# A two-layer decoder trunk: wide products in the query and query-key projections, and a new order of products within a block

## The chip, the cores and the metric

The kernel runs on one core of a Trainium2 chip. The time is device microseconds of one execution. The engines of a core are named as in the profile: PE (TensorE, matrix products) with PEld (its weight loads), DVE (VectorE), ACT (ScalarE), POOL (GpSimd) and SP (SyncE, which issues the loads of weights). SBUF is the memory the engines work from, PSUM the one in which PE sums its products.

## The reference

256 tokens of width 1024 pass two layers. Layer 0 mixes tokens by a recurrence and by retention, layer 1 by differential attention; both go on with a cross-attention into 256 memory tokens and an MLP of width 4096. What matters here, cut to the lines:

```python
# layer 1's mixing
q, k, v = jnp.split(h @ w_in, 3, axis=-1)          # 1024 columns each
...
# both layers
q = (h @ w_q).reshape(bsz, s, X_HEADS, X_HEAD_DIM)
k, v = jnp.split(mem_n @ w_kv, 2, axis=-1)
logits = jnp.einsum('bshd,bmhd->bhsm', q, k).astype(jnp.float32) * (X_HEAD_DIM ** -0.5)
p = jax.nn.softmax(logits, axis=-1)
o = jnp.einsum('bhsm,bmhd->bshd', p.astype(v.dtype), v)
return o.reshape(bsz, s, D_MODEL) @ w_o
...
# both layers
jnp.square(jax.nn.relu(h @ w1)) @ w2
```

## The kernel before

**Products in parts.** Most products are made of two parts of each operand, a high part hi (the value rounded to the type that PE multiplies) and a low part lo (the rest). A product is the sum of three: hi by hi, lo by hi, hi by lo. `split` makes the parts: ACT copies the source into hi, DVE subtracts hi from the source. Both operations have line L129 for every operand.

**Weights.** `wpiece` (L138) loads a piece of 512 KB into `raw` (4 buffers) and splits it into `hi` and `lo` (3 buffers each), at a high priority in the scheduler, which places them ahead of other work that is ready on ACT and DVE. A piece is one block: 128 output columns over all 1024 input rows. A split of 128x1024 can begin when the block three places before has released its buffers.

**Two ways to project.** The activations are held transposed, columns are tokens: `xh` and `xl` of 128 x 8 x 256. `proj_cols` (L163) takes two blocks into one PSUM tile `mm` of 128x512, 256 columns a block: per block and each of the 8 slices kt of the input, three products of 256 columns (narrow: `mm<-xhl,hi`, `mm<-xhl,lo`, `mm<-xhl,hi`), 24 in all. Then one call of `evac` empties the tile. `proj_wide` (L308) takes one block into one tile of 128x512. The hi weights of a slice are multiplied with both parts of the activations in one product of 512 columns (wide), so that hi by hi is summed in the left half and hi by lo in the right half of the tile; the lo weights are multiplied with xh in a narrow product, into the left half. A block has 8 wide and 8 narrow products. Its emptying has to add the halves. In the MLP, `up` (L1003) uses it: ACT copies the right half to `ul` (L1009), DVE adds the left half and `ul` (L1010). A block that comes first after the activations are made (`opening`) is made of 24 narrow products in another order, in both ways.

**Where they are used.** `proj_wide` is used by the MLP's first half in both layers, 32 blocks each, on tiles that alternate between the pools `mm` and `tr` (two buffers each). `proj_cols` is used by `q_proj` in the cross-attention (L924, 4 calls of two blocks per layer) and by the query-key projection of layer 1's differential attention (L1115 and L1116, 8 calls). In layer 0, `q_proj`'s tile is copied whole to `qT` (L927); in layer 1 it is split into two parts `qT`. In the differential attention L1115 and L1116 copy the tile to `qTd` and `kTd`.

**What lies around.** `q_proj` calls alternate with `softmax` of the heads whose queries are ready: scores `acc<-KT,qT`, their maximum and exponential, the reciprocal, the transpositions (`tr`), and the copy or split of the transposed into `PT`. Ahead of it the keys and values of the memory are projected into `mm` tiles; in both layers the last key tile is split into `KT1h` and `KT1l`, and in layer 1 the values are split into `Vs`. In the differential attention each second pair of blocks is followed by `heads` (scores `acc`, a biased copy `z`, maximum, exponential, a weighted difference, transposition `tr`, copy `PTd`).

**What sets the order.** A scheduler places the instructions of each engine in a fixed order from their dependencies and priorities; an engine takes its own in that order. `mm` chains the products of one PSUM bank, so that one sum is not mixed with another. The PSUM pools `acc`, `mm` and `tr` give their buffers in turn: a tile waits until the last reader of the tile two turns before is done (`mm`, `tr`).

Of the kernel before, what the change touches and what calls it, by code (L numbers as in the profile page):

```python
# [8 lines left out]
F32 = mybir.dt.float32  # L9
F32R = mybir.dt.float32r  # L10
AF = mybir.ActivationFunctionType
ALU = mybir.AluOpType
# [25 lines left out]
def kernel(ctx: ExitStack, tc: tile.TileContext, ins: dict, out: bass.AP):  # L38
    nc = tc.nc
    I = ins  # L40
# [5 lines left out]
    const = ctx.enter_context(tc.tile_pool(name="const", bufs=1))  # L46
# [21 lines left out]
    def nm(s):  # L68
        cnt[0] += 1
        return f"{s}_{cnt[0]}"  # L70
# [4 lines left out]
    def mm_t():  # L75
        return ps_mm.tile([128, 512], F32, tag="mm", name=nm("mm"))
# [42 lines left out]
    def mm(o, lhsT, rhs, start, stop):  # L119

        ins = nc.tensor.matmul(o, lhsT=lhsT, rhs=rhs, start=start, stop=stop)  # L121
        key = o.tensor.name
        prev = last_in_bank.get(key)
        if prev is not None:
            behind(ins, prev, "one accumulation group per bank")
        last_in_bank[key] = ins

    def split(hi, lo, src):
        return nc.scalar.activation(hi, src, AF.Copy), nc.vector.tensor_tensor(lo, src, r32(hi), op=ALU.subtract)  # L129
# [178 lines left out]
    def proj_wide(w, blk, xT, ps, opening=False):  # L308

        xh, xl = xT  # L310
        wh, wl = wpiece(w[blk].rearrange("p (kt c) -> p kt c", kt=8), 8, 128)
        if opening:
            for k0 in (0, 4):
                for kt in range(k0, k0 + 4):
                    mm(ps[:, 0, :], lhsT=wh[:, kt, :], rhs=xh[:, kt, :], start=(kt == 0), stop=False)
                    mm(ps[:, 0, :], lhsT=wl[:, kt, :], rhs=xh[:, kt, :], start=False, stop=False)
                for kt in range(k0, k0 + 4):
                    mm(ps[:, 0, :], lhsT=wh[:, kt, :], rhs=xl[:, kt, :], start=False, stop=(kt == 7))
            return False
        for kt in range(8):  # L320
            if kt == 7:
                mm(ps[:, 0, :], lhsT=wl[:, kt, :], rhs=xh[:, kt, :], start=False, stop=False)
            mm(ps, lhsT=wh[:, kt, :], rhs=xT.both[:, kt, :, :], start=(kt == 0), stop=(kt == 7))
            if kt < 7:
                mm(ps[:, 0, :], lhsT=wl[:, kt, :], rhs=xh[:, kt, :], start=False, stop=False)
        return True

    def load_mem(pool):
        mh = pool.tile([128, 8, 256], F32R, tag="memh", name="memh")
# [25 lines left out]
    xT = xt(xpool, "A")  # L355
# [3 lines left out]
    omu = const.tile([128, 14], F32, name="omu")  # L359
    behind(nc.vector.tensor_scalar(omu, prm[:, R_MU:R_MU + 14], -1.0, 1.0, op0=ALU.mult, op1=ALU.add), d1[1], "the activations first")  # L360
    oka = const.tile([128, 4], F32, name="oka")
    const.tile([128, 22], F32, name="pad")

    quad = const.tile([128, 2], F32, name="quad")
    for q in range(4):
# [59 lines left out]
    for b0 in (0, 2):  # L425
# [6 lines left out]
        for j in range(2):  # L432
            b = b0 + j
# [29 lines left out]
    for hf in range(2):  # L463
        for b in range(4):
            mm(pss[:, 0:16].rearrange("p (f h b) -> p f b h", f=2, h=2)[:, hf, b, :],
               lhsT=kk2[:, b, hf * 128:(hf + 1) * 128], rhs=hsel, start=True, stop=True)
# [39 lines left out]
    kT = tok_major(kt_.rearrange("p (b g) t -> p b (g t)", b=4), "kT")  # L506
# [393 lines left out]
    def cross(layer, KT, V, after, mid=lambda: None):  # L900
# [21 lines left out]
        oT = next_xT()  # L922

        def q_proj(c):  # L924
            def ev(ps):
                if layer == 0:
                    nc.scalar.activation(qT[:, 2 * c:2 * c + 2, :], ps, AF.Copy)  # L927
                else:
                    split(qT[0][:, 2 * c:2 * c + 2, :], qT[1][:, 2 * c:2 * c + 2, :], ps)
            proj_cols(I["w_q"][layer], 2 * c, xT, ev, c == 0)  # L930

        def softmax(hp, t):
            ps = acc_t().rearrange("p (h m) -> p h m", h=2)
# [126 lines left out]
    def diff(before, after):  # L1060
# [51 lines left out]
                nc.scalar.activation(PT[:, hd, t * 128:t * 128 + n], pt[:, :n], AF.Copy)  # L1112

        for c in range(4):
            proj_cols(I["w_dqk"], 2 * c, xT, lambda ps, c=c: nc.scalar.activation(qT[:, 2 * c:2 * c + 2, :], ps, AF.Copy), c == 0)  # L1115
            proj_cols(I["w_dqk"], 8 + 2 * c, xT, lambda ps, c=c: nc.scalar.activation(kT[:, 2 * c:2 * c + 2, :], ps, AF.Copy))  # L1116
            if c > 0:
                heads(2 * c - 2)
                heads(2 * c - 1)
# [186 lines left out]
```

## Time and profile before

| what | value |
|---|---|
| runs | 902.22, 899.11, 898.23 us; median 899.11 |
| profiled execution | 897.66 us, its span 895.9 us |
| granted clock of PE, mean | 0.995 |
| instructions in the span | 14122 |
| PE, PEld busy | 876.5, 752.6 us (98%, 84%) |
| DVE, ACT busy | 593.5, 454.9 us (66%, 51%) |
| POOL busy | 30.5 us (3%) |
| HBM read | 148.01 MB, 168 GB/s over the span |

The span runs from the first to the last instruction that the profiler records; the time of an execution holds a little more. PE's records overlap, since the next product enters while the last is still leaving: the time that one takes from the engine is the distance between the starts of two (its pitch), not its duration. A number in brackets behind a row is the idle time of the engine just before it, with what ended it.

By place: layer 0's query projection lies from about 274 to 302 us, its MLP from 340 to 520, layer 1's query-key projection from 530 to 587, its values and output from 587 to 640, its query projection from 649 to 676, its MLP from 712 to 882.

### The profile page before, as it was taken

The page shows a single profiled execution, that of the slowest core. Times are in us where ns is not written, and L with a number is a line of the kernel's source. Part 1 is how long each engine was busy: PE and PEld are TensorE (multiplying, and loading weights), DVE is VectorE, ACT ScalarE, POOL GpSimd, SP SyncE. Part 2 cuts the span into 40 slices and gives each one's busy share as a digit, 9 for nine tenths or more (in the row PEclk, how much of TensorE's full clock was granted, in tenths as well). Part 3 has the DMA queues.
Part 4 walks back from the last instruction along what each step waited for, and adds up shares of the span by engine and source line. Part 5 has one row for each costly group of instructions (what it writes and reads, how often), then busy time and mean ns, then how long its engine had stood idle before and what let it go on. Part 6 is the DMA issues. An engine that isn't in the chain of part 4 may idle for free.

```text
span 895.9 us, 14122 instructions
## 1 busy us (share of the span) xinstructions
PE 876.5 (98%) x5546; PEld 752.6 (84%) x5546; DVE 593.5 (66%) x937; ACT 454.9 (51%) x730; POOL 30.5 (3%) x51
## 2 busy tenths in 40 slices
PE   7999999999999999999999999999999999999996
PEld 5988889777889889888888889978899888888885
DVE  4669888455476557666666675786776676666665
ACT  5765444324465436444444454674564554444443
POOL 2000000001000100000000000001000000000001
PEclk8999999999999999999999999999999999999999
DMA  9754433222656545565555555443563465655551
GB/s 310 237 152 129 140 120 119 72 72 95 198 203 213 185 168 191 195 190 192 193 189 189 188 175 180 142 124 113 170 203 97 153 198 188 188 189 191 188 189 66
DMA packets 47078, 149.98 MB, mean 167 GB/s; under 512 B 4731, under 2 KB 4900, under 8 KB 46884
## 3 DMA queue, kind: packets, MB, share of 16 engines
q1 hardware_dynamic: 45456, 142.73, 49.2%
q10 hardware_dynamic: 1108, 3.72, 1.2%
q0 software_dynamic: 448, 2.63, 0.8%
q8 instruction: 43, 0.70, 0.3%
q14 instruction: 23, 0.19, 0.1%
HBM read 148.01 MB, written 2.63 MB: 168 GB/s over the span
## 4 chain that ended last, share of the span: by engine, by line
PE 90%; DVE 4%; issue 2%; ACT 2%; POOL 1%; DMA 1%; POOLq 0%; SPq 0%; DVEq 0%; ACTq 0%
PE mm L121 37%; PE acc L121 35%; PE tr L121 15%; DVE lo L129 1%; PE tr L254 1%; ACT hi L129 1%; DMA h<-in_x_dram 1%; PE tr L1111 1%; PE tr L958 1%; DVE z L1092 0%; PE acc L254 0%; POOL rs L226 0%; DVE xn L268 0%; PE tr L500 0%; POOL xn L1189 0%
## 5 line engine op out<-in xcount | busy, mean ns | idle before, releaser
L129 DVE TENSOR_TENSOR lo<-raw,hi 128x1024 fp32r<-128x1024 f32 x262 | 320.0, 1223 | 213.3 <-ACT hi L129 211.1
L129 ACT ACTIVATE hi<-raw 128x1024 fp32r<-128x1024 f32 x262 | 277.6, 1060 | 333.5 <-PE mm L121 122.5
L121 PE MATMUL mm<-xhl,hi 128*128 128x256 f32 (+1 forms) x784 | 188.0, 319 | 1.3 <-ACT xhl L129 1.1
L121 PEld LDWEIGHTS mm<-xhl,hi 128*128 128x128 f32 x784 | 129.7, 189 | 12.1 <-ACT xhl L129 2.0
L121 PE MATMUL mm<-xhl,lo 128*128 128x256 f32 x512 | 138.1, 282 | 0.0
L121 PE MATMUL acc<-hi,hl 128*128 128x512 f32 x256 | 100.2, 391 | 0.0
L121 PE MATMUL acc<-hi,hh 128*128 128x512 f32 x256 | 100.1, 391 | 0.0
L121 PE MATMUL acc<-lo,hh 128*128 128x512 f32 x256 | 99.6, 389 | 0.0
L121 PEld LDWEIGHTS mm<-xhl,lo 128*128 128x128 f32 x512 | 96.6, 189 | 2.5
L121 PE MATMUL tr<-xhl,hi 128*128 128x512 f32 x256 | 92.8, 395 | 0.0
L121 PE MATMUL acc<-hi,xhl 128*128 128x512 f32 x256 | 81.9, 396 | 0.0
L121 PE MATMUL tr<-xhl,lo 128*128 128x256 f32 x256 | 66.7, 281 | 0.0
L121 PEld LDWEIGHTS acc<-hi,hl 128*128 128x128 f32 x256 | 48.0, 188 | 11.3 <-DVE hl L129 0.9
L121 PEld LDWEIGHTS acc<-lo,hh 128*128 128x128 f32 x256 | 48.1, 188 | 10.4
L121 PEld LDWEIGHTS acc<-hi,xhl 128*128 128x128 f32 x256 | 47.7, 188 | 9.7
L121 PEld LDWEIGHTS acc<-hi,hh 128*128 128x128 f32 x256 | 48.1, 188 | 8.8
L121 PEld LDWEIGHTS tr<-xhl,hi 128*128 128x128 f32 x256 | 48.2, 188 | 8.5
L121 PEld LDWEIGHTS tr<-xhl,lo 128*128 128x128 f32 x256 | 48.2, 188 | 2.9
L121 PE MATMUL acc<-lo,xhl 128*128 128x512 f32 x128 | 50.4, 394 | 0.0
L121 PE MATMUL mm<-memh,hi 128*128 128x256 f32 x128 | 37.0, 289 | 0.0
L121 PE MATMUL mm<-meml,hi 128*128 128x256 f32 x128 | 36.8, 288 | 0.0
L121 PE MATMUL mm<-memh,lo 128*128 128x256 f32 x128 | 36.5, 285 | 0.0
(303 smaller groups left out, 1369.5 us busy)
## 6 DMA issues: line engine op xcount, KB each, us to landing
raw<-in_w_dram SPq DMA_DIRECT2D x64, 512.0 KB, 4.3
raw<-in_mlp_w_dram SPq DMA_DIRECT2D x64, 512.0 KB, 4.3
raw<-in_hyb_w_in_dram SPq DMA_DIRECT2D x16, 512.0 KB, 3.7
raw<-in_w_k_dram SPq DMA_DIRECT2D x16, 512.0 KB, 3.5
raw<-in_xattn_w_kv_dram SPq DMA_DIRECT2D x16, 512.0 KB, 3.7
raw<-in_w_q_dram SPq DMA_DIRECT2D x16, 512.0 KB, 4.0
raw<-in_xattn_w_o_dram SPq DMA_DIRECT2D x16, 512.0 KB, 3.5
raw<-in_w_dqk_dram SPq DMA_DIRECT2D x16, 512.0 KB, 3.6
```

Source lines behind the costliest of these rows:

```text
L121: ins = nc.tensor.matmul(o, lhsT=lhsT, rhs=rhs, start=start, stop=stop)
L129: return nc.scalar.activation(hi, src, AF.Copy), nc.vector.tensor_tensor(lo, src, r32(hi), op=ALU.subtract)
L254: nc.tensor.transpose(ps[:, k4, :], x[:, kt * 128:(kt + 1) * 128], ident)
L958: nc.tensor.transpose(pt[:, j, m, :], P[:, j, m * 128:(m + 1) * 128], ident)
L1111: nc.tensor.transpose(pt[:, k * 128:(k + 1) * 128], z3[:, 0, k * 128:(k + 1) * 128], ident)
```

## The change

Three things are edited. First, `proj_wide` no longer alternates: it issues seven of the eight wide products, then the eight narrow ones, then the last wide one. Second, a new helper `proj_two` makes two blocks with `proj_wide`, each in an `mm` tile of its own, and hands the left half and the copied right half `ul` to a function `dst`; `q_proj` in both layers and the query-key projection use it in place of `proj_cols`. `summed_to` adds the halves on DVE, or copies an opening block on ACT. In layer 1's `q_proj` the sum is written back to `ul` and then split. With 8 blocks per layer in `q_proj` and 16 in the query-key projection, less the three opening ones, 29 blocks become wide. Third, an unused pad of 22 columns becomes one of 16.

```diff
--- before.py
+++ after.py
@@ -317,13 +317,29 @@
                 for kt in range(k0, k0 + 4):
                     mm(ps[:, 0, :], lhsT=wh[:, kt, :], rhs=xl[:, kt, :], start=False, stop=(kt == 7))
             return False
+        for kt in range(7):
+            mm(ps, lhsT=wh[:, kt, :], rhs=xT.both[:, kt, :, :], start=(kt == 0), stop=False)
         for kt in range(8):
-            if kt == 7:
-                mm(ps[:, 0, :], lhsT=wl[:, kt, :], rhs=xh[:, kt, :], start=False, stop=False)
-            mm(ps, lhsT=wh[:, kt, :], rhs=xT.both[:, kt, :, :], start=(kt == 0), stop=(kt == 7))
-            if kt < 7:
-                mm(ps[:, 0, :], lhsT=wl[:, kt, :], rhs=xh[:, kt, :], start=False, stop=False)
+            mm(ps[:, 0, :], lhsT=wl[:, kt, :], rhs=xh[:, kt, :], start=False, stop=False)
+        mm(ps, lhsT=wh[:, 7, :], rhs=xT.both[:, 7, :, :], start=False, stop=True)
         return True
+
+    def proj_two(w, blk, xT, pool, dst, opening=False):
+
+        for b in range(2):
+            ps = mm_t().rearrange("p (x t) -> p x t", x=2)
+            if proj_wide(w, blk + b, xT, ps, opening and b == 0):
+                ul = pool.tile([128, 256], F32, tag="ul", name=nm("ul"), bufs=2)
+                nc.scalar.activation(ul, ps[:, 1, :], AF.Copy)
+                dst(b, ps[:, 0, :], ul)
+            else:
+                dst(b, ps[:, 0, :], None)
+
+    def summed_to(o, p, ul):
+        if ul is None:
+            nc.scalar.activation(o, p, AF.Copy)
+        else:
+            nc.vector.tensor_tensor(o, p, ul, op=ALU.add)
 
     def load_mem(pool):
         mh = pool.tile([128, 8, 256], F32R, tag="memh", name="memh")
@@ -359,7 +375,7 @@
     omu = const.tile([128, 14], F32, name="omu")
     behind(nc.vector.tensor_scalar(omu, prm[:, R_MU:R_MU + 14], -1.0, 1.0, op0=ALU.mult, op1=ALU.add), d1[1], "the activations first")
     oka = const.tile([128, 4], F32, name="oka")
-    const.tile([128, 22], F32, name="pad")
+    const.tile([128, 16], F32, name="pad")
 
     quad = const.tile([128, 2], F32, name="quad")
     for q in range(4):
@@ -922,12 +938,16 @@
         oT = next_xT()
 
         def q_proj(c):
-            def ev(ps):
+            def dst(b, p, ul):
+                i = 2 * c + b
                 if layer == 0:
-                    nc.scalar.activation(qT[:, 2 * c:2 * c + 2, :], ps, AF.Copy)
+                    summed_to(qT[:, i, :], p, ul)
+                elif ul is None:
+                    split(qT[0][:, i, :], qT[1][:, i, :], p)
                 else:
-                    split(qT[0][:, 2 * c:2 * c + 2, :], qT[1][:, 2 * c:2 * c + 2, :], ps)
-            proj_cols(I["w_q"][layer], 2 * c, xT, ev, c == 0)
+                    summed_to(ul, p, ul)
+                    split(qT[0][:, i, :], qT[1][:, i, :], ul)
+            proj_two(I["w_q"][layer], 2 * c, xT, cp, dst, c == 0)
 
         def softmax(hp, t):
             ps = acc_t().rearrange("p (h m) -> p h m", h=2)
@@ -1112,8 +1132,8 @@
                 nc.scalar.activation(PT[:, hd, t * 128:t * 128 + n], pt[:, :n], AF.Copy)
 
         for c in range(4):
-            proj_cols(I["w_dqk"], 2 * c, xT, lambda ps, c=c: nc.scalar.activation(qT[:, 2 * c:2 * c + 2, :], ps, AF.Copy), c == 0)
-            proj_cols(I["w_dqk"], 8 + 2 * c, xT, lambda ps, c=c: nc.scalar.activation(kT[:, 2 * c:2 * c + 2, :], ps, AF.Copy))
+            proj_two(I["w_dqk"], 2 * c, xT, dp, lambda b, p, ul, c=c: summed_to(qT[:, 2 * c + b, :], p, ul), c == 0)
+            proj_two(I["w_dqk"], 8 + 2 * c, xT, dp, lambda b, p, ul, c=c: summed_to(kT[:, 2 * c + b, :], p, ul))
             if c > 0:
                 heads(2 * c - 2)
                 heads(2 * c - 1)
```

The program's rows on PE fall from 4276 to 3161 in the listing (equal neighbours are counted in one row), those on ACT grow from 611 to 635 and on DVE from 911 to 944; POOL and SP stay as they are. Names carry buffer numbers here; the numbers differ between the two programs.

PE, the second half of a block of the MLP's `up` in layer 0, and the start of the next, before:

```order
L121 MATMUL mm_801_4823<-xhl_519_3470,hi_803_4825 128x512
L121 MATMUL mm_801_4823<-xhl_519_3470,lo_804_4826 128x256
L121 MATMUL mm_801_4823<-xhl_519_3470,hi_803_4825 128x512
L121 MATMUL mm_801_4823<-xhl_519_3470,lo_804_4826 128x256 x2
L121 MATMUL mm_801_4823<-xhl_519_3470,hi_803_4825 128x512
L121 MATMUL tr_806_4849<-xhl_519_3470,hi_808_4851 128x512
L121 MATMUL tr_806_4849<-xhl_519_3470,lo_809_4852 128x256
L121 MATMUL tr_806_4849<-xhl_519_3470,hi_808_4851 128x512
```

The same block and the next one in the change:

```order
L121 MATMUL mm_831_4883<-xhl_530_3436,hi_833_4885 128x512 x7
L121 MATMUL mm_831_4883<-xhl_530_3436,lo_834_4886 128x256 x8
L121 MATMUL mm_831_4883<-xhl_530_3436,hi_833_4885 128x512
L121 MATMUL tr_836_4909<-xhl_530_3436,hi_838_4911 128x512 x7
L121 MATMUL tr_836_4909<-xhl_530_3436,lo_839_4912 128x256 x8
L121 MATMUL tr_836_4909<-xhl_530_3436,hi_838_4911 128x512
```

The alternation is gone, and between two blocks eight wide products follow one another: the last of one block and the seven of the next.

ACT at the start of the query-key projection, before (`hi<-raw` is the weight split, L1115 and L1116 empty a pair of blocks):

```order
L129 ACTIVATE hi_877_5270<-raw_876_5269 128x1024
L129 ACTIVATE hi_881_5302<-raw_880_5301 128x1024
L1115 ACTIVATE qTd_5170<-mm_865_5176 128x512
L129 ACTIVATE hi_884_5332<-raw_883_5331 128x1024
L129 ACTIVATE hi_888_5364<-raw_887_5363 128x1024
L1116 ACTIVATE kTd_5171<-mm_872_5238 128x512
```

And in the change (L333 is the copy of a right half in `proj_two`, L340 the copy of the opening block):

```order
L340 ACTIVATE qTd_5136<-mm_876_5142 128x256
L129 ACTIVATE hi_897_5254<-raw_896_5253 128x1024
L333 ACTIVATE ul_884_5197<-mm_880_5174 128x256
L129 ACTIVATE hi_902_5280<-raw_901_5279 128x1024
L333 ACTIVATE ul_889_5223<-mm_885_5200 128x256
L129 ACTIVATE hi_907_5306<-raw_906_5305 128x1024
L333 ACTIVATE ul_894_5249<-mm_890_5226 128x256
L129 ACTIVATE hi_912_5332<-raw_911_5331 128x1024
```

There is now one copy of 256 columns for each block, behind a weight split each time; on DVE the add of the block stands behind the low part of the same split.

DVE in layer 1's query projection, from the reciprocal of the first softmax to the split of the third pair of blocks, before (`lo` is the weight split, `PT` the split of the transposed, `qT` that of the queries):

```order
L952 RECIPROCAL rc_1168_6697<-sm_1167_6694 128x2
L954 TENSOR_SCALAR xn_1166_6693<-xn_1166_6693,rc_1168_6697 128x256 x2
L129 TENSOR_TENSOR lo_1189_6835<-raw_1187_6833,hi_1188_6834 128x1024
L129 TENSOR_TENSOR PT_1148_6549<-tr_1169_6701,PT_1147_6548 128x2x2x128
L952 RECIPROCAL rc_1174_6728<-sm_1173_6725 128x2
L954 TENSOR_SCALAR xn_1172_6724<-xn_1172_6724,rc_1174_6728 128x256 x2
L129 TENSOR_TENSOR lo_1212_6993<-raw_1210_6991,hi_1211_6992 128x1024
L129 TENSOR_TENSOR PT_1148_6549<-tr_1175_6732,PT_1147_6548 128x2x2x128
L129 TENSOR_TENSOR qT_1144_6537<-mm_1176_6739,qT_1143_6536 128x512
```

And in the change (`ul<-mm,ul` adds the halves of a block, `qT<-ul,qT` is its split; mm_1215 and mm_1220 are the fifth and the sixth block, and the seventh takes the buffer of the fifth):

```order
L129 TENSOR_TENSOR lo_1233_6709<-raw_1231_6707,hi_1232_6708 128x1024
L972 RECIPROCAL rc_1207_6580<-sm_1206_6577 128x2
L974 TENSOR_SCALAR xn_1205_6576<-xn_1205_6576,rc_1207_6580 128x256 x2
L972 RECIPROCAL rc_1213_6611<-sm_1212_6608 128x2
L974 TENSOR_SCALAR xn_1211_6607<-xn_1211_6607,rc_1213_6611 128x256 x2
L129 TENSOR_TENSOR lo_1257_6862<-raw_1255_6860,hi_1256_6861 128x1024
L129 TENSOR_TENSOR PT_1182_6441<-tr_1208_6584,PT_1181_6440 128x2x2x128
L129 TENSOR_TENSOR PT_1182_6441<-tr_1214_6615,PT_1181_6440 128x2x2x128
L342 TENSOR_TENSOR ul_1219_6645<-mm_1215_6622,ul_1219_6645 128x256
L342 TENSOR_TENSOR ul_1224_6673<-mm_1220_6650,ul_1224_6673 128x256
L129 TENSOR_TENSOR qT_1178_6429<-ul_1219_6645,qT_1177_6428 128x256
```

Both `PT` now stand together, behind the second reciprocal and the weight split lo_1257, which belongs to the piece three places after the sixth block; the adds of the fifth and the sixth block follow both `PT`.

## Rows read from the trace of the kernel before

**Rows 1.** The page, part 1: engine, busy us (share of the span), instructions.
```profile
PE 876.5 (98%) x5546; PEld 752.6 (84%) x5546; DVE 593.5 (66%) x937; ACT 454.9 (51%) x730; POOL 30.5 (3%) x51
```

**Rows 2.** The page, part 4: share of the span by engine in the chain that ended last.
```profile
PE 90%; DVE 4%; issue 2%; ACT 2%; POOL 1%; DMA 1%; POOLq 0%; SPq 0%; DVEq 0%; ACTq 0%
```

**Rows 3.** Busy time by stretch: one with heads, and one around layer 1's queries.
```profile
560.00:575.00 15.00, 14.52 (x121) 13.31 (x119) 11.76 (x33) 9.72 (x29) 0.00 (x0) 1.00 0.48 141
640.00:690.00 50.00, 50.00 (x394) 47.61 (x393) 38.00 (x65) 31.02 (x58) 1.08 (x2) 1.00 0.44 147
```

**Rows 4.** Timeline of PE, query-key projection: start us, us, line, operation, out<-in, count.
```profile
534.07 0.28 PE L121 MATMUL mm<-xhl,lo 128*128 128x256 f32 x1
...
537.98 0.28 PE L121 MATMUL mm<-xhl,lo 128*128 128x256 f32 x1
```

**Rows 5.** The chain, layer 0's MLP: start us, us, what.
```profile
354.27 5.47 PE acc L121 x24
359.75 2.81 PE mm L121 x16
362.56 2.82 PE tr L121 x16
365.38 5.44 PE acc L121 x24
```

**Rows 6.** The chain, layer 1's MLP.
```profile
739.07 2.80 PE mm L121 x16
...
744.66 5.49 PE acc L121 x24
```

**Rows 7.** Timelines of PE, ACT and DVE at a block's end in layer 0's MLP.
```profile
362.16 0.40 PE L121 MATMUL mm<-xhl,hi 128*128 128x512 f32 x1
362.40 0.40 PE L121 MATMUL tr<-xhl,hi 128*128 128x512 f32 x1
...
362.65 1.06 ACT L129 ACTIVATE hi<-raw 128x1024 fp32r<-128x1024 f32 x1 [1.75 <-PE mm L121]
363.61 0.37 ACT L1009 ACTIVATE ul<-mm 128x256 f32<-128x256 f32 x1
...
363.74 1.22 DVE L129 TENSOR_TENSOR lo<-raw,hi 128x1024 fp32r<-128x1024 f32 x1 [1.59 <-ACT hi L129]
364.88 0.41 DVE L1010 TENSOR_TENSOR rl<-mm,ul 128x256 f32<-128x256 f32 x1
```

**Rows 8.** Timelines of DVE and PE: a z of the heads and the transposition on it.
```profile
558.63 0.34 DVE L1108 SCALAR_TENSOR_TENSOR z<-z,cf 128x128 f32<-128x128 f32 x1
...
559.03 0.33 PE L1111 MATMUL tr<-prm,z 128*128 128x128 f32 x1 [0.44 <-DVE z L1108]
```

**Rows 9.** Timelines of PE and DVE, start of layer 0's query projection.
```profile
275.68 0.88 PE L121 MATMUL mm<-xhl,hi 128*128 128x256 f32 x6
...
276.62 0.68 DVE L129 TENSOR_TENSOR KT1l<-mm,KT1h 128x512 fp32r<-128x512 f32 x1
```

**Rows 10.** Timelines of DVE and PE behind the last query-key block.
```profile
584.25 1.22 DVE L129 TENSOR_TENSOR lo<-raw,hi 128x1024 fp32r<-128x1024 f32 x1
...
586.14 1.16 PE L121 MATMUL acc<-kTd,qTd 64*128 64x128 f32 x8 [0.58 <-DVE z L1092]
```

**Rows 11.** Timelines of PE and DVE, layer 1's query projection.
```profile
651.52 0.87 PE L121 MATMUL mm<-xhl,hi 128*128 128x256 f32 x6
...
652.20 0.68 DVE L129 TENSOR_TENSOR KT1l<-mm,KT1h 128x512 fp32r<-128x512 f32 x1
...
671.21 1.23 DVE L129 TENSOR_TENSOR lo<-raw,hi 128x1024 fp32r<-128x1024 f32 x1 [0.55 <-ACT hi L129]
672.35 0.68 DVE L129 TENSOR_TENSOR PT<-tr,PT 128x512 fp32r<-128x512 f32 x1
672.96 0.68 DVE L129 TENSOR_TENSOR qT<-mm,qT 128x512 fp32r<-128x512 f32 x1
```

## The prediction

> **What bounds the kernel.** I read the page first: PE is busy 98% of the span [rows 1], and PE is 90% of the chain that ended last [rows 2]. The next number matters as much: in the stretch 640 to 690, where layer 1's query projection lies, PE is busy 50.00 of 50.00 us [rows 3]. So whatever PE is made to wait there, or spared, goes into the time one to one. DVE and ACT are busy 66% and 51% as an average [rows 1]. That says little about a single block of weights, so I then read the pitches of PE [rows 4 to 6], the emptying of one block's tile [rows 7] and the places where DVE holds several things in line [rows 9 to 11].
>
> Pitches come from starts, since the ends of matmuls are modelled. In the query-key projection 33 narrow products lie between 534.07 and 537.98 [rows 4]: 3.91 / 33 = 118.5 ns, so a block of 24 costs 2.845 us. A stretch of 24 products of 512 columns takes 5.44 to 5.47 us in layer 0's MLP [rows 5] and 5.49 in layer 1's [rows 6]: 227 and 229 ns. An alternating block (8 wide and 8 narrow) takes 2.81 and 2.80 us [rows 5, 6].
>
> The forecast is made against the profiled execution: 897.66 us, span 895.9. The median of the three runs is 899.11, which is 1.45 higher, and that is added at the end. A measurement of this kernel can tell about 0.5% (4.5 us) from no change.
>
> **The order of a wide block.** Seven wide, eight narrow, one wide. If what costs is the alternation, the block costs the sum of the two pitches: 8 x 0.227 + 8 x 0.1185 = 2.76 us against 2.81 (layer 0), and 8 x 0.229 + 8 x 0.1185 = 2.78 against 2.80 (layer 1). There are 31 wide up blocks in a layer, so 31 x 0.053 + 31 x 0.022 = **-2.3 us**. No row shows seven wide products followed by eight narrow ones. The ends: 0 (the 5.4 ns a pair are not the alternation's) and -3.1 (both layers gain 0.05). I take the middle because both parts were measured, if apart. Evacuation in the MLP stays covered: its tiles alternate between two pools, so four blocks are in flight.
>
> **29 blocks made wide.** On PE each goes from 2.845 to 2.76: 29 x 0.08 = -2.3 us if nothing waits. Here something does. Before, two blocks shared one mm tile and one ACT copy of 512 columns emptied it. Now each block has a tile of its own, and there are two mm tiles: block n+2 may start only when block n is emptied, by a copy on ACT and then an add on DVE.
>
> That this chain is too long can be read from the MLP, whose emptying is the same [rows 7]. The block's last product starts at 362.16 and the next block's first at 362.40 by its pitch; ACT takes the next weight split first (362.65, 1.06 us), then the copy (363.61, 0.37); DVE takes the low part of the split first (363.74, 1.22), then the add (364.88, 0.41), which ends at 365.29. From the pitch end, 362.39, that is 2.90 us. PE follows a DVE result by 0.06 (z ends at 558.97, the transposition starts at 559.03 [rows 8]). So block n+2 starts 2.96 us after block n ends, not 2.76: two blocks take 2.96 + 2.76 = 5.72 us, one 2.86. Against 2.845 the gain is gone: **the wide blocks save nothing in steady state**, +0.015 each. The weight splits stay ahead of the copies and adds in the new order on both engines, so the MLP's chain is the right one.
>
> **Layer 0's queries.** The second block now needs the other mm tile, last read by the subtraction KT1l, which runs 276.62 to 277.30 [rows 9]. The six products from 275.68 are the opening block's last four and the next block's first two [rows 9], so that PE comes to the second block at 275.68 + 4 x 0.12 = 276.16 and stands about 1.2 us. DVE and ACT catch up in it, the next five blocks run nearer 2.76 than 2.86, and 0.5 comes back: **+0.7**. Ends: -0.6 (seven blocks at -0.08, no wait) and +1.3.
>
> **Query-key projection.** 15 blocks. The first seven have nothing else on DVE: +0.2. Then the heads come between, where DVE is busy 11.76 of 15 us [rows 3], and four adds of 0.41 join per stretch. An add that stands behind a weight split (1.22 us) or behind the z chain delays the tile; I count one delay of 0.6, half a split, in each of the two stretches that follow: +1.2. At the tail PE already waits 0.58 us for a z that stands behind a split (584.25, 1.22) [rows 10]; the last block's add joins that line with 0.41 and its copy before it: +0.6. Sum **+2.0**, ends 0 and +4.5 (a full 1.22 at each of three places and 0.8 at the tail).
>
> **Layer 1's queries.** Here the result is split again, so DVE has two operations a block and ACT two. Three waits:
> - the second block waits for KT1l (652.20 + 0.68 = 652.88); PE comes to it at 651.52 + 4 x 0.12 = 652.0 [rows 11]: +0.95;
> - the third waits for the opening block's subtraction, which in the new DVE order stands behind four subtractions of the values and a split: +0.6, half a split;
> - the seventh waits for the add of the fifth. In the order it stands behind a weight split that begins only when the sixth block ends, and behind both subtractions PT of the softmax. From the sixth block's end: 0.26 until ACT starts, 1.09 until DVE starts its part (362.65 to 363.74 [rows 7]), 1.14 for that, 0.61 for each PT (672.35 to 672.96 [rows 11]) and 0.41 + 0.06: 4.2 us. Two groups of transpositions cover 0.6 of it: +3.6.
>
> Less 7 x 0.08 = 0.56 and with 0.1 of steady drift: 0.95 + 0.6 + 3.6 - 0.56 + 0.1 = **+4.7**. Ends: -0.6 (all hidden) and +6.5 (the third block waits for a full split, the eighth for another).
>
> The remaining edits cost nothing: the pad's width moves tiles in SBUF only, and weight loads (512 KB each) are as many as before and are issued as early.
>
> Sum: -2.3 + 0.7 + 2.0 + 4.7 = +5.1. Then 897.66 + 5.1 + 1.45 = **904.2 us**, slower by 0.6%.
>
> **Rivals.**
> - A, not slower: the emptying hides. The point that decides is 2.96 against 2.76: were the chain 0.2 us shorter (the copy and the add taken ahead of the next split, or ACT let go earlier because the last high product comes sooner), a tile would be free when PE comes. Each block then saves 0.08, and the order of work on DVE in layer 1 would have slack as well. -2.3 - 2.3 = -4.6: 894.5 us. For it: ACT is idle 1.75 us before the split [rows 7]. Against: both engines take the split first, in order. 0.15.
> - B, the waits are small: heads cost 0, the seventh block's wait is half, 1.8, because PT's source is ready earlier than I place it. -2.3 + 0.7 + 0 + 2.9 = +1.3: 900.4. For it: DVE is not full there, it stood 0.55 us before the split at 671.21 [rows 11]. Against: that idle time itself ends with ACT's half of the split, on which the add would wait too. 0.26.
> - C, the order does nothing, so that edit does not do what it should: the MLP stays at 2.81, the rest as forecast. +7.4: 906.5. 0.12. For it: the wide pitch of 227 was taken from products with other operands. The Trainium skill, "TensorE: Matmul & The Clock Gate", section Back-to-back issue gap, gives an isolated warm gap of N / 2.4 + 2.5 ns in which the neighbour plays no part; by it three narrow products take 327.5 ns and a wide with a narrow 325, so that 29 blocks would gain 0.6 us and the order none. The rows disagree in size: 355.5 and 351 ns [rows 4, 5].
> - D, DVE becomes the bound between heads: three stretches 1.9 us longer each in place of 0.6, 908. Against: 11.76 + 1.66 = 13.4 of 15 still fits. 0.07.
>
> **How the numbers follow.** The forecast has 0.40. The range leaves out A (0.15) and the ends beyond D: 897.0 to 908.5. With 899.11 as the middle, faster means under 894.6 and slower over 903.6. Faster: most of A, 0.13. Same: the rest of A, nearly all of B, and those sums of the forecast that end under 903.6 (0.15 of its 0.40): 0.42. Slower: the rest of the forecast (0.25), C, D, a trace of B: 0.45.
>
> **What would show it.** MLP blocks at 2.76 instead of 2.81 us would confirm the order; 2.81 means C. In the query-key projection, starts of blocks 2.86 us apart, with PE idle 0.1 to 0.2 at each block and the add as releaser, would confirm the chain; 2.76 without idle means A. In layer 1's queries the seventh block should start some 4.8 us later than now, after an idle stretch of about 3.6 whose releaser is the add; without that stretch the forecast falls. PE's busy time should fall by about 5 us while the span grows.

## The result, and the profile after

| | before | changed |
|---|---|---|
| median of 5 runs each | 898.44 us (898.04 to 902.22) | 906.39 us (905.64 to 908.09) |
| ratio, 95% interval | | 1.0083 (1.006 to 1.0105) |
| profiled execution: span | 895.9 us | 904.2 us |

The change makes the kernel slower by 8 us. The 906.39 us lie in the range of 897.0 to 908.5, and 2.2 beyond the 904.2 of the forecast. As a difference it is off by more, +8.0 measured for +5.1, since the kernel before has come out 0.7 faster here than the 899.11 that the forecast started from. The page of the changed kernel, parts 1 and 4:

```profile
PE 879.9 (97%) x5314; PEld 742.0 (82%) x5314; DVE 603.4 (67%) x970; ACT 458.9 (51%) x753; POOL 31.0 (3%) x51
...
PE 86%; DVE 7%; issue 3%; ACT 3%; POOL 1%; DMA 1%; POOLq 0%; SPq 0%; DVEq 0%; ACTq 0%
```

PE is a little busier in microseconds and less as a share: 97% where [rows 1] has 98%. In the chain DVE has 7% where [rows 2] has 4%, and PE 86% for 90%. Work that used to lie beside PE now stands in front of it.

To see where, I cut the span at the norm transpositions (line L254), which open a cross-attention, an MLP and the differential attention in turn. Timeline of PE, the first of them at each place, before:

```profile
263.06 0.66 PE L254 MATMUL tr<-prm,xn 128*128 128x128 f32 x4
...
334.36 0.60 PE L254 MATMUL tr<-prm,xn 128*128 128x128 f32 x4
...
523.21 1.04 PE L254 MATMUL tr<-prm,xn 128*128 128x128 f32 x8
...
640.62 0.60 PE L254 MATMUL tr<-prm,xn 128*128 128x128 f32 x4
...
706.95 0.60 PE L254 MATMUL tr<-prm,xn 128*128 128x128 f32 x4
```

And in the changed kernel:

```profile
262.80 0.66 PE L254 MATMUL tr<-prm,xn 128*128 128x128 f32 x4
...
336.43 0.60 PE L254 MATMUL tr<-prm,xn 128*128 128x128 f32 x4
...
524.45 1.04 PE L254 MATMUL tr<-prm,xn 128*128 128x128 f32 x8
...
643.03 0.60 PE L254 MATMUL tr<-prm,xn 128*128 128x128 f32 x4
...
715.52 0.60 PE L254 MATMUL tr<-prm,xn 128*128 128x128 f32 x4
```

The differences of the starts give the stages, here with those of the experiments below (the last column runs to the end of the span, all of it us):

| kernel | layer 0 cross-attention | layer 0 MLP | differential attention | layer 1 cross-attention | layer 1 MLP, end |
|---|---|---|---|---|---|
| before | 71.30 | 188.85 | 117.41 | 66.33 | 188.95 |
| changed | 73.63 | 188.02 | 118.58 | 72.49 | 188.68 |
| order_only | 71.28 | 188.02 | 117.51 | 66.34 | 188.76 |
| old_order | 73.70 | 188.85 | 118.44 | 72.66 | 188.89 |
| q1_pairs | 73.58 | 188.05 | 118.56 | 66.30 | 188.70 |
| first_pair | 72.49 | 188.02 | 118.51 | 69.78 | 188.68 |
| four_tiles | 71.18 | 188.05 | 117.01 | 68.61 | 188.69 |
| first_empty | 72.18 | 188.00 | 116.32 | 68.03 | 188.74 |
| keep_busy | 73.62 | 188.06 | 118.61 | 71.31 | 188.72 |
| dqk_first | 71.24 | 187.97 | 116.56 | 66.35 | 188.66 |
| again (changed) | 73.56 | 188.01 | 118.54 | 72.52 | 188.65 |
| pair_again (first_pair) | 72.25 | 188.07 | 118.59 | 71.34 | 188.72 |

A stage that an edit does not touch repeats within 0.25 us, so that the table reads differences of a few tenths. The one exception is layer 1's cross-attention in first_pair and pair_again, the same kernel twice; there the granted clock differed, as told below. What lies ahead of the first cut moves by up to 5 us between these traces for reasons of its own, and is left out. Of the 8.3 us between the two spans, 2.33 lie in layer 0's cross-attention, 1.17 in the differential attention, 6.16 in layer 1's cross-attention; the MLPs give back 0.83 and 0.27, the start 0.26.

**The MLP.** The chain in both layers:

```profile
361.78 2.77 PE mm L121 x16
364.55 2.79 PE tr L121 x16
367.35 5.46 PE acc L121 x24
...
753.23 5.47 PE acc L121 x24
758.69 2.80 PE mm L121 x16
761.49 2.81 PE tr L121 x16
```

Layer 0's blocks take 2.77 and 2.79 us where [rows 5] has 2.81 and 2.82; the products behind them take 5.46 where it has 5.44 to 5.47. In layer 1 a block takes 2.80 as before [rows 6], and the 0.27 us that this stage gives back come from the products behind the blocks (16 times 0.02), 5.47 where [rows 6] has 5.49.

**Layer 0's queries.** Timeline of PE before, the scores behind the last block:

```profile
302.27 3.67 PE L121 MATMUL acc<-KT,qT 128*128 128x256 f32 x16
```

Timelines of PE and DVE in the changed kernel:

```profile
277.19 1.83 PE L121 MATMUL mm<-xhl,hi 128*128 128x512 f32 x7 [1.19 <-DVE KT1l L129]
...
305.82 0.42 DVE L342 TENSOR_TENSOR qT<-mm,ul 128x256 f32<-128x256 f32 x1
307.03 1.29 DVE L964 TENSOR_REDUCE mx<-acc 128x2 f32<-128x512 f32 x2 [0.79 <-PE acc L121]
...
303.39 2.75 PE L121 MATMUL acc<-KT,qT 128*128 128x256 f32 x12
...
306.29 1.13 PE L121 MATMUL acc<-KT,qT 128*128 128x256 f32 x4
```

The second block waits for KT1l as foreseen (1.19). The second thing was not: the last block's sum is ready at 305.82 + 0.42 = 306.24, and the last four of the 16 score products start at 306.29, so that the maximum starts at 307.03. Counted from the first cut, the last block ends at 39.21 before (302.27) and at 40.59 now (303.39), 1.38 later; the other 0.95 of the 2.33 us lie behind it.

**Query-key projection.** Timelines of DVE, of PE's weight loads (PEld) and of PE:

```profile
539.50 0.42 DVE L342 TENSOR_TENSOR qTd<-mm,ul 128x256 f32<-128x256 f32 x1
...
539.97 1.47 PEld L121 LDWEIGHTS mm<-xhl,hi 128*128 128x128 f32 x7 [0.25 <-DVE qTd L342]
...
566.39 0.70 PE L121 MATMUL mm<-xhl,hi 128*128 128x512 f32 x2 [0.57 <-DVE qTd L342]
```

A block's weights are loaded 0.05 us after the add of the block two places before it. It is the wait that the prediction read from the MLP; here it leaves the weight loads idle for 0.25. Further on, score products that the scheduler now places between blocks stand in that gap; the longest wait left is 0.57.

**Layer 1's queries.** Timelines of PE and DVE:

```profile
655.43 1.87 PE L121 MATMUL mm<-xhl,hi 128*128 128x512 f32 x7 [0.89 <-DVE KT1l L129]
...
659.21 1.88 PE L121 MATMUL mm<-xhl,hi 128*128 128x512 f32 x7 [0.26 <-DVE qT L129]
...
677.73 2.11 PE L121 MATMUL mm<-xhl,hi 128*128 128x512 f32 x7 [2.54 <-DVE ul L342]
...
681.35 2.59 PE L121 MATMUL mm<-xhl,hi 128*128 128x512 f32 x8
...
684.97 0.27 PE L121 MATMUL acc<-KT1h,qT 128*128 128x256 f32 x1
...
674.83 1.23 DVE L129 TENSOR_TENSOR lo<-raw,hi 128x1024 fp32r<-128x1024 f32 x1
675.97 1.28 DVE L129 TENSOR_TENSOR PT<-tr,PT 128x512 fp32r<-128x512 f32 x2
677.16 0.75 DVE L342 TENSOR_TENSOR ul<-mm,ul 128x256 f32<-128x256 f32 x2
```

All three waits are there with the releasers that were forecast: KT1l, the opening block's subtraction, the add of the fifth block. The third shows the line on DVE: weight split, two PT, then the adds (two of 0.42 in one row, the first ends at 677.58), and PE starts 0.15 us after that one. And the windows of the changed kernel from there on (the number after POOL is the granted clock):

```profile
677.70:681.40 3.70, 3.67 (x16) 3.33 (x17) 0.97 (x3) 0.67 (x2) 0.00 (x0) 0.70 0.29 117
681.40:685.00 3.60, 3.60 (x19) 3.04 (x19) 1.56 (x2) 1.64 (x3) 0.00 (x0) 0.83 0.00 0
685.00:688.00 3.00, 3.00 (x27) 3.00 (x26) 1.99 (x3) 1.58 (x4) 0.00 (x0) 1.00 0.49 180
```

The seventh and eighth block, 677.73 to 684.97, take 7.24 us. For part of it the granted clock is down: 0.70 and 0.83 as means of the two windows, that is a mix of the levels of 2.4 and 1.2 GHz, and 1.00 again behind them.

### The profile page after: what moved, and what is told of

Read it like the earlier page. It is cut to its first block, busy times and chain, and to the rows that moved or that the text cites. A ratio compares the mean times of both kernels' runs of the same rounds, so it can differ in the third digit from the quotient of the medians.

```text
span 904.2 us, 13749 instructions
## 1 busy us (share of the span) xinstructions
PE 879.9 (97%) x5314; PEld 742.0 (82%) x5314; DVE 603.4 (67%) x970; ACT 458.9 (51%) x753; POOL 31.0 (3%) x51
## 4 chain that ended last, share of the span: by engine, by line
PE 86%; DVE 7%; issue 3%; ACT 3%; POOL 1%; DMA 1%; POOLq 0%; SPq 0%; DVEq 0%; ACTq 0%
PE acc L121 35%; PE mm L121 34%; PE tr L121 15%; DVE lo L129 2%; ACT hi L129 1%; PE tr L254 1%; POOL rs L226 1%; DMA h<-in_x_dram 1%; ACT xn L969 1%; DVE xn L268 0%; PE tr L516 0%; PE acc L254 0%; PE tr L1131 0%; DVE mx L964 0%; POOL xn L1209 0%
## 5 line engine op out<-in xcount | busy, mean ns | idle before, releaser
L121 PE MATMUL mm<-xhl,hi 128*128 128x512 f32 (+1 forms) x552 | 146.6, 384 | 6.6 <-DVE ul L342 2.5
L121 PEld LDWEIGHTS mm<-xhl,hi 128*128 128x128 f32 x552 | 99.9, 190 | 26.4 <-issue 5.1
L121 PEld LDWEIGHTS mm<-xhl,lo 128*128 128x128 f32 x512 | 72.7, 191 | 5.0
L121 PE MATMUL mm<-xhl,lo 128*128 128x256 f32 x512 | 76.7, 284 | 0.0
L121 PE MATMUL tr<-xhl,hi 128*128 128x512 f32 x256 | 69.9, 394 | 0.0
L121 PEld LDWEIGHTS tr<-xhl,lo 128*128 128x128 f32 x256 | 34.9, 189 | 2.7
L121 PE MATMUL tr<-xhl,lo 128*128 128x256 f32 x256 | 35.5, 282 | 0.0
```

## The experiments

My theory: the loss comes from the emptying of wide blocks, that is from where the copy and the add stand in the lines of ACT and DVE; the new order of products is a small gain; behind layer 1's standstill a low clock adds to it. Rivals: each wide block costs its share wherever it stands; DVE simply has too much to do; two tiles are too few and the lines don't matter. Ratios are to the runs of the kernel before on the same chip.

**order_only**: the kernel before with the new order in `proj_wide`.

```diff
-        for kt in range(8):
-            if kt == 7:
...
+        for kt in range(7):
+            mm(ps, lhsT=wh[:, kt, :], rhs=xT.both[:, kt, :, :], start=(kt == 0), stop=False)
         for kt in range(8):
+            mm(ps[:, 0, :], lhsT=wl[:, kt, :], rhs=xh[:, kt, :], start=False, stop=False)
+        mm(ps, lhsT=wh[:, 7, :], rhs=xT.both[:, 7, :, :], start=False, stop=True)
```

> The kernel before with the new order of products within a wide block and nothing else; the projections keep their pairs of narrow blocks. My theory (the order saves a little in layer 0's MLP, nothing in layer 1's; all the loss comes from the emptying of wide blocks): a pair of up blocks in layer 0 falls from 5.63 us to 5.56, in layer 1 it stays at 5.60, the time is 898.4 - 1.1 = 897.3. Rival (the order is nothing, or what fell in the MLP is given back at the next products): 898.4, pairs as before.

897.54 us against 898.38, ratio 0.9991 (0.9981 to 1.0). The time alone hardly tells the order from nothing, the stages do: layer 0's MLP is 0.83 shorter, just as in the changed kernel, layer 1's 0.19. The order is a gain of about 1 us, as expected.

**old_order**: the changed kernel with the alternating order put back (the same diff, reversed).

> The changed kernel with the alternating order of products put back everywhere. My theory (order and projections add up): 906.4 + 1.0 = 907.4, and the seventh query block of layer 1 waits 2.5 us as in the changed kernel. Rival (the run of seven wide products helps the waits, because the low weights are needed later): 909 or more, with new waits for lo of about 0.3 us a block.

907.49 us, ratio 1.0102 (1.0088 to 1.0116), near the 907.4 expected. The MLPs are back at 188.85 and 188.89, the projections lose what they lost, and the seventh block of layer 1 waits 2.54 us again: the two edits add up, and the order is not what hurts.

**q1_pairs**: the changed kernel, layer 1's query projection on pairs of narrow blocks.

```diff
         def q_proj(c):
...
+            if layer == 1:
+                proj_cols(I["w_q"][layer], 2 * c, xT, lambda ps: split(qT[0][:, 2 * c:2 * c + 2, :], qT[1][:, 2 * c:2 * c + 2, :], ps), c == 0)
+                return
             proj_two(I["w_q"][layer], 2 * c, xT, cp, dst, c == 0)
```

> The changed kernel with layer 1's query projection taken back to pairs of narrow blocks. My theory (of the 8 us lost, about 6 are in layer 1's queries: the seventh block's wait and a low clock behind it): 906.4 - 6.2 = 900.2, and the granted clock stays 1.00 around the seventh block. Rival (each wide block of a projection costs about the same 0.27 us, wherever it stands): 906.4 - 7 x 0.27 = 904.5.

900.74 us, ratio 1.0025 (1.0012 to 1.0038). Timeline of PE, the two cuts around the stage:

```profile
644.40 0.60 PE L254 MATMUL tr<-prm,xn 128*128 128x128 f32 x4
...
710.70 0.60 PE L254 MATMUL tr<-prm,xn 128*128 128x128 f32 x4
```

66.30 us, as before, with the other stages as in the changed kernel and the granted clock at 1.00 throughout the stage. Seven of 29 blocks hold about 6 of 8 us; an even cost per block is out.

**first_empty**: copy and add of the projections' blocks, and in layer 1's queries the split of the sum, at the priority of the weight splits.

```diff
                 ul = pool.tile([128, 256], F32, tag="ul", name=nm("ul"), bufs=2)
-                nc.scalar.activation(ul, ps[:, 1, :], AF.Copy)
-                dst(b, ps[:, 0, :], ul)
+                with tc.high_priority():
+                    nc.scalar.activation(ul, ps[:, 1, :], AF.Copy)
+                    dst(b, ps[:, 0, :], ul)
```

> The changed kernel with the copy and the add of the projections' wide blocks at the scheduler's high priority, so that in layer 1's queries they stand ahead of the weight splits and of the softmax's subtractions. My theory (the place in DVE's and ACT's line is what PE waits for): the seventh block's wait falls from 2.54 us to 0.3 or less, the clock stays 1.00, 901.5 us with 1 to either side. Rival (DVE has too much to do there, the order only moves the wait): 905 to 907, with another wait of 2 us or more near by.

898.73 us, ratio 1.0 (0.9991 to 1.0009): nearly the whole loss is gone, 3 us more than expected. Timelines of PE and DVE in layer 1's queries:

```profile
651.33 1.87 PE L121 MATMUL mm<-xhl,hi 128*128 128x512 f32 x7 [0.89 <-DVE KT1l L129]
...
655.31 1.90 PE L121 MATMUL mm<-xhl,hi 128*128 128x512 f32 x7 [0.47 <-DVE ul L343]
...
670.42 0.40 DVE L343 TENSOR_TENSOR ul<-mm,ul 128x256 f32<-128x256 f32 x1
...
671.30 1.23 DVE L129 TENSOR_TENSOR lo<-raw,hi 128x1024 fp32r<-128x1024 f32 x1
672.44 0.42 DVE L129 TENSOR_TENSOR qT<-ul,qT 128x256 fp32r<-128x256 f32 x1
672.78 1.28 DVE L129 TENSOR_TENSOR PT<-tr,PT 128x512 fp32r<-128x512 f32 x2
```

The operations on DVE are the same ones; the adds (670.42 here) now stand ahead of the weight split and both PT. The seventh block waits for nothing, and no low clock follows. So it was the place in the line, not the amount of work. What I had not counted on: the differential attention falls to 116.32, 1.1 us below that of the kernel before. The waits for KT1l stay, and the third block of layer 1 waits a little longer, 0.47 for 0.26. In layer 0 the scores behind the last block (timeline of PE):

```profile
302.45 3.61 PE L121 MATMUL acc<-KT,qT 128*128 128x256 f32 x16
```

All 16 run in a row again, for the add of the last block now ends 1.0 us behind that block in place of 2.9. The block ends 0.81 later than before, counted from the first cut, and the stage is 0.88 longer: what lay behind the last block is gone.

**four_tiles**: the projections' blocks on tiles from two pools in turn.

```diff
-            ps = mm_t().rearrange("p (x t) -> p x t", x=2)
+            ps = (mm_t, tr_t)[b]().rearrange("p (x t) -> p x t", x=2)
```

> The changed kernel with the projections' wide blocks on tiles that alternate between mm and tr, as in the MLP: four tiles in place of two. My theory (the line on DVE and ACT is the cause in layer 1, the number of tiles only the place where it shows): the waits for KT1l are gone in both layers, but a block now needs the tr tile of a transposition and waits about 2.3 us for the subtraction PT in the same line: 903.8, with 2 us to either side. Rival (two tiles are too few and that is all): no wait of over 0.5 us in either query projection, 897 to 898.

899.37 us, ratio 1.0015 (1.0005 to 1.0025). It lies between the two, but outside my range and much nearer to the rival: 4.4 below my number, 1.4 above the rival's 898. Timelines of DVE and PE in layer 1's queries:

```profile
670.73 1.23 DVE L129 TENSOR_TENSOR lo<-raw,hi 128x1024 fp32r<-128x1024 f32 x1
671.88 1.28 DVE L129 TENSOR_TENSOR PT<-tr,PT 128x512 fp32r<-128x512 f32 x2
...
672.62 1.90 PE L121 MATMUL tr<-xhl,hi 128*128 128x512 f32 x7 [1.49 <-DVE PT L129]
```

The wait did move to PT in the same line, but is 1.49 us where I had put 2.3, and no low clock came behind it. In layer 0 four tiles leave no wait that the timeline shows in the query projection: 71.18, as before. In layer 1, 2.3 us of the loss stay, this wait among them. So I was wrong to call the number of tiles only the place where the loss shows: with the copy and the add placed as before, four tiles take off 7.0 of the 8 us. Most of the loss needs both, an add that stands late in its line and no more than two tiles to wait for.

**first_pair**: the first two query blocks of both layers as a pair.

```diff
+            if c == 0:
+                proj_cols(I["w_q"][layer], 2 * c, xT, ev, True)
+                return
             proj_two(I["w_q"][layer], 2 * c, xT, cp, dst, c == 0)
```

Here `ev` is the emptying of the kernel before.

> The changed kernel with the first two query blocks of both layers taken back to one tile and a pair of narrow blocks, so that the second block needs no tile that KT1l still reads. My theory (these two waits, 1.19 and 0.89 us, are a loss of their own): they are gone, two blocks lose their 0.08, the seventh block's wait and the low clock stay: 906.4 - 1.9 = 904.5. Rival (the later waits take them up, since DVE had used the standstill to catch up): 906 or more, the third or seventh block waits longer by as much.

904.11 us, ratio 1.0065 (1.0049 to 1.0081), near the 904.5 expected. The two waits for KT1l are gone and no other took up more than about 0.2 of them: layer 0's stage is 1.14 shorter, and the standstill before the seventh block is 2.54 us as it was. Against my expectation no low clock came behind that standstill in this trace (windows: from the seventh block on, and a stretch ahead of the first cut):

```profile
679.60:683.00 3.40, 3.32 (x18) 2.94 (x19) 1.03 (x3) 0.95 (x3) 0.00 (x0) 1.00 0.32 127
...
160.00:260.00 100.00, 99.99 (x790) 78.11 (x789) 50.82 (x81) 37.23 (x53) 3.32 (x3) 0.95 0.36 117
```

The two blocks start at 679.68 and end at 685.38: 5.70 us. This execution had its low clock elsewhere, 0.95 between 160 and 260, where the work is the same in all of these kernels.

**keep_busy**: 14 products that nobody reads, ahead of layer 1's seventh block.

```diff
+            if layer == 1 and c == 3:
+                fill = acc_t()
+                for _ in range(14):
+                    mm(fill, lhsT=xT[0][:, 0, :128], rhs=xT.both[:, 0, :, :], start=True, stop=True)
             proj_two(I["w_q"][layer], 2 * c, xT, cp, dst, c == 0)
```

> The changed kernel with 14 products of 512 columns that nobody reads, into a score tile, ahead of layer 1's seventh query block, so that PE does not stand there. My theory (the seventh and the eighth block took 3.62 us each because the granted clock had fallen after the standstill): they take 2.76 each, 1.7 us come back, the extra products cost about 0.5 elsewhere: 905.2. Rival (the two blocks were slow for another reason, weights that came late or a port): still 3.6 each, 906.9 or more.

904.59 us, ratio 1.0076 (1.0053 to 1.0099). Timeline of PE, seventh block to the first score behind the eighth:

```profile
677.64 1.86 PE L121 MATMUL mm<-xhl,hi 128*128 128x512 f32 x7 [0.68 <-DVE ul L342]
...
680.29 2.03 PE L121 MATMUL mm<-xhl,hi 128*128 128x512 f32 x8
...
683.34 0.28 PE L121 MATMUL acc<-KT1h,qT 128*128 128x256 f32 x1
```

And the window:

```profile
678.00:682.00 4.00, 4.00 (x23) 3.42 (x22) 0.92 (x3) 1.55 (x3) 0.00 (x0) 1.00 0.19 79
```

More work on PE, and the stage is 1.2 us shorter (71.31 for 72.49). The medians, 904.59 and 906.39, say the same, but the single runs overlap (904.03 to 908.67 and 905.64 to 908.09) and so do the intervals of the ratios; the stage is the evidence. The wait for the add is still there (0.68 behind the last extra product), but the two blocks take 5.70 us where the changed kernel has 7.24, at a granted clock of 1.00. The 1.5 us were the clock's.

**again** and **pair_again**: the changed kernel and first_pair once more, one trace each.

> The changed kernel once more, for its trace alone. Open is whether the granted clock falls behind the 2.54 us standstill in each execution: it did in the trace of the changed kernel, not in that of first_pair with the same standstill. If the standstill decides, the seventh and the eighth block take 3.6 us each again; if it depends on more than the standstill, they may take 2.76.

> first_pair once more, for its trace alone: blocks of 2.8 us behind the standstill, as in its first trace, if its two waits less ahead of it are what kept the clock; 3.6 us if the executions differ.

906.42 and 903.28 us, one run each. The window behind the standstill in the changed kernel:

```profile
678.10:681.80 3.70, 3.69 (x16) 3.32 (x17) 0.96 (x3) 0.66 (x2) 0.00 (x0) 0.70 0.24 92
```

And in first_pair:

```profile
676.20:678.90 2.70, 2.70 (x11) 2.41 (x11) 0.00 (x0) 0.00 (x0) 0.00 (x0) 0.50 0.00 0
```

Both have it low this time, 0.70 and 0.50. In the second trace of first_pair the two blocks take 7.23 us (674.78 to 682.01), in the first 5.70: the same program with the same standstill, and layer 1's cross-attention is 71.34 in the one and 69.78 in the other. This is the price of the low clock with nothing else changed, 1.5 us. Of five traces with a standstill of 2.5 us there (the changed kernel twice, old_order with 0.64 from 680 to 684, first_pair twice), four show the fall behind it. What spares the fifth stays open. The Trainium skill ("TensorE: Matmul & The Clock Gate", Part 1) says of the slow products at a kernel's start that their number differed from run to run of the same kernel. The two traces of first_pair differ in the same way, behind a standstill in place of the start.

**dqk_first**: first_empty with both query projections as before, so that wide blocks stay in the query-key projection alone.

```diff
-            proj_two(I["w_q"][layer], 2 * c, xT, cp, dst, c == 0)
+            proj_cols(I["w_q"][layer], 2 * c, xT, ev, c == 0)
```

> The new order, the wide blocks in the query-key projection alone, their copy and add at high priority, and both query projections as pairs of narrow blocks as before. My theory (wide blocks pay where their emptying stands first in line and nothing else needs DVE at once): the stretch of differential attention is 1.1 us shorter than before, the MLPs 1.0, nothing is lost elsewhere: 898.4 - 2.1 = 896.3. Rival (the shorter stretch in one trace is chance): the same as the new order alone, 897.4.

895.77 us (895.17 to 896.36), ratio 0.9969 (0.9958 to 0.998): faster than the kernel before and the changed one. Timeline of PE, the two cuts around the differential attention:

```profile
521.83 1.04 PE L254 MATMUL tr<-prm,xn 128*128 128x128 f32 x8
...
638.39 0.60 PE L254 MATMUL tr<-prm,xn 128*128 128x128 f32 x4
```

116.56 us, 0.85 below the kernel before; with 0.88 and 0.29 from the MLPs it makes 2.0 us. By the medians it is 2.8 (895.77 for 898.56).

## Why the prediction was right, and where its sizes were off

- **The whole**: the stages that lose and the one that gains were foreseen. Of the four terms, -2.3, +0.7, +2.0 and +4.7, the runs showed -1.1, +2.3, +1.2 and +6.2: three errors in one direction, of which the query-key projection took back 0.8.
- **What bounds**: PE waits one to one. It held: the wait of 1.19 that first_pair took out of layer 0's queries made its stage 1.14 shorter, and the two waits of layer 1 that went with it, 0.89 and 0.26, made theirs 1.15 shorter in pair_again, where the clock fell as in the changed kernel (71.34 for 72.49).
- **The order of a wide block**, -2.3: the sign held, the size was half, -1.1. Layer 0 gains 0.83 (0.07 a pair of blocks, less 0.02 that the products behind it give back) and layer 1 0.19 in order_only. The failing step is the sum of two pitches that were measured apart. It holds to 0.02 us in layer 0 (2.77 and 2.79 for 2.76); in layer 1 a block stays at 2.80 where the sum gave 2.78.
- **Rival C, and the gap rule of the Trainium skill** that stood beside it (page "TensorE: Matmul & The Clock Gate", section Back-to-back issue gap): with the neighbour playing no part the order would do nothing. Layer 1's block agrees with that, layer 0's (2.81 to 2.77) does not. That C's 906.5 is the number nearest to 906.39 is luck: the order did gain 1.1, and two of the three other terms that C took over were too small.
- **The saving of a wide block on PE**, 0.08: it is not the same in every stage. In first_empty, in stretches without a wait, a wide block has a pitch of 2.79 us in layer 0's queries (299.42 to 302.21), 2.81 in the query-key projection (535.00 to 551.85, six blocks) and 2.82 in layer 1's queries (672.86 to 675.68). A narrow one before has 2.88 in layer 0's queries (69 products from 276.40 to 284.68) and 2.85 in the other two. So 0.09, 0.04 and 0.03 are saved, about 1.4 us over the 29 blocks where the prediction had 2.3.
- **The emptying chain**, 2.96 us from a block's end to the next start on its tile: it held. The query-key projection shows it, and first_empty and four_tiles, which shorten it or give it room, take most of the waits away.
- **Layer 0's queries**, +0.7: measured 2.33. The wait for KT1l was right (1.2). Two steps failed. That 0.5 would come back was wrong: the last block ends 1.4 late. And I followed the sum only as something that sets a tile free, not as data that somebody reads: before, one ACT copy gave the scores their last queries; now they wait for copy and add. Another 0.95 us lies there, behind the last block. first_pair and first_empty tell the two apart: in first_pair the wait for KT1l is gone and the stage is still 1.2 longer than before, 0.9 of it behind the last block; in first_empty, where the add ends early, 0.07 is left there.
- **Query-key projection**, +2.0: measured 1.17. A delay of 0.57 and small ones, not 0.6 at each of three places; score products stand in some of the gaps.
- **Layer 1's queries**, +4.7: measured 6.16. The mechanism and all three places were right, and the seventh block starts 4.5 us after the sixth block ends, where 4.2 was worked out. The idle time of 2.54 in the row is less than the 3.6 forecast, since a second wait of 0.34 and the tails of the records lie beside it: the two groups of transpositions take some 0.8 (0.46 and 0.35 by the starts before, 667.78 to 668.24 and 670.59 to 670.94), which leaves 3.7 of the 4.5. What was missed is the 1.5 us of low clock behind the standstill. Nothing in the sum had a price for that. Without it the rest comes to 4.6, near the 4.7, but partly by luck: the third block waits 0.26 and not 0.6, and seven wide blocks save 0.2 and not 0.56.
- **PE's busy time** was to fall by about 5 us and rose by 3.4 (879.9). As a check it was badly chosen. A record of a wide product lasts 0.40 us, and the next one starts 0.24 us after its start [rows 7], so about the first 0.16 us of a wait count as busy; and products at the low clock count as busy for longer.
- **Rival A**: its deciding point, the emptying taken ahead of the split, is first_empty. Even so the time is 898.7 and not 894.5: the waits for KT1l (1.17 and 0.89) don't depend on it, the third block of layer 1 waits 0.47, the order gains 1.1 and not 2.3, and the wide blocks save 1.4 and not 2.3. B and D are out: layer 1's waits were whole, and DVE was in the wrong order rather than full.

## What to carry to other kernels

A wide block saved PE 0.03 to 0.09 us here and added an operation to the emptying of its tile. What that costs depends on the line in which the operation stands and on how many tiles there are to go on with: moving it ahead in the line took off 7.7 us, two more tiles 7.0. Follow the operation in the order of its engine, and ask of it both who waits for the tile and who waits for the data. The 15 wide blocks of the query-key projection lost 1.17 us in the changed kernel; with copy and add ahead of the weight splits they gained 0.85 (dqk_first). And price a standstill of PE by what follows it too: here 2.5 us cost up to 4.

## What the runs showed of the hardware that was not expected

- In layer 1's queries PE had only eight small transpositions to do over 4.5 us, and nothing in the last 2.5 of them. Behind that the granted clock fell in four of five traces, and two blocks took 7.2 us in place of 5.70. Behind a standstill of 1.49 us (four_tiles, one trace) it did not fall.
- Products that nobody reads, put into that standstill, kept the granted clock at 1.00 and made the stage 1.2 us shorter (71.31 for 72.49).
- The new order shortens a block in layer 0's MLP and not in layer 1's, with the same instructions: seven wide products in a row have a pitch of 226 to 230 ns in the one (361.62 to 363.20 and 364.39 to 366.00) and 233 in the other (758.53 to 760.16). Why is open.
